# S5 parameters kept on chip, raw gates in DRAM, and another preparation of y in a two-layer trunk on one Trainium2 core

## The chip, the core and the metric

The kernel runs on one core of one Trainium2 chip. The metric is the time of one execution on the device, in microseconds (us). TensorE (PE) does the matmuls, VectorE (DVE), ScalarE (ACT) and GpSimd (POOL) the element-wise work, and SyncE (SP) issues most of the DMAs; ScalarE issues a few. Each engine runs its own instructions in the order in which they stand in its program, and waits at one until the semaphores it needs are there; so does SP with its DMAs.

## What is computed

Two layers over x of 1024 frames by 1024 channels, all fp32. Layer 0 is an S5 state-space mixer with a GLU behind it, layer 1 a spatial gating unit.

```python
for i in range(DEPTH):                      # DEPTH = 2
    h = rmsnorm(x, norm_g[i])
    if i % 2 == 0:
        branch, gate = jnp.split(h @ s5_w_in[j], 2, axis=-1)
        y = jax.nn.gelu(s5_mixer(branch, A_re, A_im, log_dt, B_re, B_im, C_re, C_im, D))
        y = y * jax.nn.sigmoid(y @ s5_w_glu[j] + s5_b_glu[j])
        out = (y * jax.nn.silu(gate)) @ s5_w_out[j]
    else:
        u, v, gate = jnp.split(h @ sgu_w_in[j], 3, axis=-1)
        y = sgu_mixer(jax.nn.gelu(u), jax.nn.gelu(v), ln_g, ln_b, w_s, b_s)
        out = (y * jax.nn.silu(gate)) @ sgu_w_out[j]
    x = x + out
return rmsnorm(x, final_g)
```

`s5_mixer` runs 64 groups of 16 channels; each drives 64 complex diagonal states (`lam_bar = exp(lam * dt)`) over the frames and gives `Re(C h) + D u`.

## The kernel before

Every large product is done in three matmuls per pair of 128-row operands, because each fp32 operand is split in a high and a low part (L104 to L106: high by high, low by high, high by low). The unit of work is a *half*: one tile of 128 output channels for 512 of the 1024 frames, 8 x 3 = 24 matmuls into one PSUM bank. A weight tile is loaded by SP into `raw` (L135), its high part is made by ScalarE (`w_hi`, L138) and its low part by VectorE or GpSimd (`w_lo`, L109).

*Stage 1* is the S5 input projection: 16 tiles of two halves. Tiles 0 to 7 are the branch, 8 to 15 the gate. `in_out` (L470) empties a bank: VectorE multiplies by the row norm `rb`; a branch half goes to `stage` and from there to DRAM (`u_d`), a gate half also goes through ScalarE's Silu (L479) and to `sg_d`. Two banks, `mm`, take turns for these halves.

The *head* of stage 1 (about the first 90 us) also loads and transposes x (`x_tiles`, `x_norm`) and makes the parameters of the state space on VectorE and GpSimd (`s5_params`): powers of `lam_bar` (`lp`), of the input weights (`mu`), phase tables (`eb`, `ea16`) and scaled B and C. They are written to DRAM (`g_d`, eight DMAs; `b_d`).

Beside the halves run 16 *units* of four groups each. `gen` makes two tables on VectorE (`wn`, `xn`) from a piece of `g_d` loaded back as `gp`, of which ScalarE copies a part to a PSUM bank (`gq`, L544). `gen_pe` transposes `wn` on PE (`wt`) and makes a strip of Toeplitz taps, `kpad`; a DMA writes it skewed to DRAM (`t_d`), another reads it back (`traw`), and ScalarE copies it in another order of columns (`toep`, L601). `ssm_in` loads `us`, multiplies on PE into a bank `rot`, rotates and scans on VectorE, GpSimd and ScalarE (`gg`, `hh`), with a second bank of `rot` for the swapped state. `ssm_out` multiplies `toep` and `xn` with `us` and `hh`; ScalarE copies the result (`ysb`) and issues its store to `y_d`.

The list `todo` sets in which order these pieces and the halves are written; a scheduler then orders each engine's instructions within the limits of the dependences, so the programs' rows shown below, not the list alone, tell what stands behind what.

*Preparation of y.* `prep(k)` loads tile k of `y_d` in one DMA (L715), applies the gelu on ScalarE in two halves (L721), and splits it into `hi` and `lo` on VectorE (L723, `sub_hi`); it also loads `sg_d[k]`, multiplies it with the gelu and writes `p_d[k]`. Tiles 0 to 2 are prepared from `todo`, in the pool `B0`; tiles 3 to 7 after the list, in `B1`, which takes the place of the units' memory.

*GLU.* For each of eight tiles: a weight tile, two halves from all eight `hi`/`lo` pairs in four `mm` banks, a sigmoid on ScalarE, a product with `p_d[i]` loaded back, and the split into `ahi`, `alo` for the output projection. Behind it come the second layer's stages.

The lines on which the order around the change rests (`EARLY` is 3, `KT` 8):

```python
    for k in range(EARLY):
        todo.append((max([t_gen] + [e[0] for e in todo if e[2:] == ("out", 2 * k + 1)]) + PREP, 9, "prep", k))
...
    for e in todo:
        run[e[2]](e[3])
    wk_cm.__exit__(None, None, None)
    held_cm.__exit__(None, None, None)
...
    w_next = in_w[16]
    for k in range(EARLY, KT):
        prep(k)
```

Of the kernel before, what the change touches and what calls it, by code (L numbers as in the profile page):

```python
# [63 lines left out]
def trunk(ctx, tc, x, norm_g, final_g, s5_w_in, A_re, A_im, log_dt, B_re, B_im, C_re, C_im,  # L64
# [209 lines left out]
    def s5_params():  # L274
# [102 lines left out]
        eb = per.tile([P, 2, 32, 17], F32, name="eb")  # L377
        ea16 = per.tile([P, 2, 32, 8], F32, name="ea16")
        te = xp.tile([P, 32, 8], F32, name="te")
        for e, size, lo in ((eb, 17, G), (ea16, 8, G + 32)):  # L380
            GP.memset(e[:, 0, :, 0:1], 1.0)
            GP.memset(e[:, 1, :, 0:1], 0.0)
            for i, a in ((0, cth), (1, sth)):
                GP.tensor_copy(e[:, i, :, 1:2], a[:, lo:lo + 32].unsqueeze(2))
            k = 1
            while k < size - 1:
                w = min(k, size - 1 - k)
                cmul(GP, e[:, 0, :, k + 1:k + 1 + w], e[:, 1, :, k + 1:k + 1 + w],
                     e[:, 0, :, 1:1 + w], e[:, 1, :, 1:1 + w],
                     e[:, 0, :, k:k + 1].broadcast_to([P, 32, w]), e[:, 1, :, k:k + 1].broadcast_to([P, 32, w]),  # L390
                     te[:, :, 0:w])
                k += w
# [579 lines left out]
```

## Time and profile before

| | us |
|---|---|
| median of 3 runs (902.65 to 907.44) | 904.67 |
| profiled execution, its own time | 903.87 |
| its span in the trace | 902.2 |
| PE busy in the span | 831.6 (92%) |
| VectorE, ScalarE, GpSimd busy | 494.1, 306.5, 233.0 |
| granted clock of PE, mean | 0.976 of full |

The time lies 1.67 us around the span. A busy share is an average over stages with different limits, so it is read stage by stage: the windows show where PE is full and where it stands. For each stretch in which it stands, the waits tell which instruction of which engine came last, and the timeline of that engine (or of SP's queue) tells what that instruction stood behind. Matmuls are pipelined: one is recorded with about 0.39 us, but the next starts 0.23 us after it at full clock.

### The profile page before, as it was taken

Reading aid. Unit: us, or ns where it says so; the run is one execution under the profiler, and the core shown is the slowest. Engines: PE = TensorE matmul, PEld = TensorE weight load, DVE = VectorE, ACT = ScalarE, POOL = GpSimd, SP = SyncE. Lnnn points to the kernel's source line nnn. Section 1 sums busy time; section 2 is a strip of 40 time slices with the busy share of each in tenths; the row PEclk is TensorE's granted clock in tenths of the full one; section 3 lists DMA queues with packets and bytes.
Section 4 is the critical chain, followed back from the end, with each engine's and each line's share of the span. In section 5 each row is a group of like instructions: output and inputs, shape, how many; then the busy total and the mean of one; then the engine's idle time right before and its main releaser. Section 6 shows DMA issues by size and latency. Waiting matters only on the chain.

```text
span 902.2 us, 10797 instructions
## 1 busy us (share of the span) xinstructions
PE 831.6 (92%) x3946; PEld 673.1 (75%) x3946; DVE 494.1 (55%) x1097; ACT 306.5 (34%) x523; POOL 233.0 (26%) x262
## 2 busy tenths in 40 slices
PE   6978988999898758999999999999999899999996
PEld 5756867777777546888888888888888688888884
DVE  3896597786575556334417721121279964552155
ACT  5511244545555545334312232221221122242122
POOL 1085875656532100000000000000016731212221
PEclk9989999999999988999999999999999999999999
DMA  9827678898776698335402231230130011352022
GB/s 247 166 94 205 193 203 240 238 237 225 224 208 199 217 379 294 111 128 186 153 14 80 94 117 47 70 94 1 37 103 1 1 47 47 139 165 69 1 94 93
DMA packets 135621, 123.24 MB, mean 137 GB/s; under 512 B 23696, under 2 KB 112784, under 8 KB 135568
## 3 DMA queue, kind: packets, MB, share of 16 engines
q1 hardware_dynamic: 123664, 107.87, 40.5%
q10 hardware_dynamic: 11904, 14.68, 4.7%
q8 instruction: 31, 0.51, 0.2%
q14 instruction: 22, 0.18, 0.1%
HBM read 75.87 MB, written 37.75 MB: 126 GB/s over the span
## 4 chain that ended last, share of the span: by engine, by line
PE 58%; DVE 15%; DMA 15%; ACT 4%; POOL 4%; SPq 3%; issue 2%; ACTq 0%; DVEq 0%; POOLq 0%
PE mm L104 18%; PE mm L106 18%; PE mm L105 18%; DMA gp<-g_d 3%; DMA c<-y_d 3%; DMA t_d<-kpad 2%; DVE lo L886 2%; PE aux L910 1%; DMA traw<-t_d 1%; DVE lo L887 1%; DMA xh<-in_x 1%; POOL w_lo L109 1%; DMA raw<-in_sgu_w_in 1%; DVE tv L560 1%; ACT c L721 1%
## 5 line engine op out<-in xcount | busy, mean ns | idle before, releaser
L104 PE MATMUL mm<-ahi,w_hi 128*128 128x512 f32 x512 | 207.9, 407 | 14.0 <-DVE stage L475 8.6
L106 PE MATMUL mm<-ahi,w_lo 128*128 128x512 f32 x512 | 205.5, 402 | 0.0
L105 PE MATMUL mm<-alo,w_hi 128*128 128x512 f32 x512 | 204.7, 400 | 0.0
L104 PEld LDWEIGHTS mm<-ahi,w_hi 128*128 128x128 f32 x512 | 98.3, 192 | 35.0 <-issue 9.2
L105 PEld LDWEIGHTS mm<-alo,w_hi 128*128 128x128 f32 x512 | 98.5, 192 | 21.1 <-issue 0.8
L106 PEld LDWEIGHTS mm<-ahi,w_lo 128*128 128x128 f32 x512 | 98.2, 192 | 21.4 <-DVE w_lo L109 0.5
L138 ACT ACTIVATE w_hi<-raw 128x1024 fp32r<-128x1024 f32 x39 | 41.2, 1057 | 113.0 <-PE mm L105 73.1
L888 POOL TENSOR_TENSOR lo<-lo,lnb 128x128 f32<-128x128 f32 x64 | 34.3, 566 | 162.6 <-DVE lo L887 162.6
L109 DVE TENSOR_TENSOR w_lo<-raw,w_hi 128x1024 fp32r<-128x1024 f32 x25 | 36.6, 1464 | 63.7 <-ACT w_hi L138 63.7
L104 PE MATMUL mm<-hi,w_hi 128*128 128x512 f32 x128 | 51.9, 416 | 15.1 <-DVE hi L723 13.3
L847 POOL TENSOR_SCALAR_AFFINE_SELECT wsn<-wsn 128x1024 f32<-128x1024 f32 x1 | 1.1, 1093 | 223.3 <-DMA wsn<-in_sgu_w_s 223.3
L105 PE MATMUL mm<-lo,w_hi 128*128 128x512 f32 x128 | 52.2, 407 | 0.0
L106 PE MATMUL mm<-hi,w_lo 128*128 128x512 f32 x128 | 51.8, 407 | 0.0
L106 PE MATMUL mm<-hi,alo 128*128 128x512 f32 x128 | 51.0, 399 | 0.0
L104 PE MATMUL mm<-hi,ahi 128*128 128x512 f32 x128 | 50.7, 396 | 0.0
L104 PE MATMUL mm<-ahi,hi 128*128 128x512 f32 x128 | 50.6, 396 | 0.0
L105 PE MATMUL mm<-lo,ahi 128*128 128x512 f32 x128 | 50.6, 395 | 0.0
L105 PE MATMUL mm<-alo,hi 128*128 128x512 f32 x128 | 50.6, 395 | 0.0
L105 PE MATMUL mm<-c,ahi 128*128 128x512 f32 x128 | 50.5, 395 | 0.0
L106 PE MATMUL mm<-c,alo 128*128 128x512 f32 x128 | 50.5, 395 | 0.0
L106 PE MATMUL mm<-ahi,lo 128*128 128x512 f32 x128 | 50.4, 395 | 0.0
L104 PE MATMUL mm<-c,ahi 128*128 128x512 f32 x128 | 50.1, 396 | 0.0
(255 smaller groups left out, 1509.8 us busy)
## 6 DMA issues: line engine op xcount, KB each, us to landing
raw<-in_sgu_w_in SPq DMA_DIRECT2D x24, 512.0 KB, 3.7
cs<-e SPq DMA_DIRECT2D x32, 256.0 KB, 4.5
t_d<-kpad SPq DMA_DIRECT2D x16, 512.0 KB, 4.6
raw<-in_s_w_in SPq DMA_DIRECT2D x15, 512.0 KB, 5.8
u_d<-stage ACTq DMA_DIRECT2D x8, 512.0 KB, 3.8
us<-u_d SPq DMA_DIRECT2D x16, 256.0 KB, 5.4
traw<-t_d SPq DMA_DIRECT2D x16, 256.0 KB, 3.0
y_d<-ysb ACTq DMA_DIRECT2D x16, 256.0 KB, 4.2
```

Source lines behind the costliest of these rows:

```text
L104: T.matmul(ps, lhsT=ah, rhs=bh, start=first, stop=False)
L105: T.matmul(ps, lhsT=ah, rhs=bl, start=False, stop=False)
L106: T.matmul(ps, lhsT=al, rhs=bh, start=False, stop=last)
L109: eng.tensor_tensor(lo, src, hi.bitcast(F32), ALU.subtract)
L138: S.activation(hi, raw, AF.Copy)
L560: V.tensor_tensor(tv, pw[1].unsqueeze(2).broadcast_to(sh), second.unsqueeze(3).broadcast_to(sh), ALU.mult)
L721: S.activation(gy.rearrange("p (c l) -> p c l", l=L), yt.rearrange("p (l c) -> p c l", l=L)[:, half * 64:(half + 1) * 64], AF.Gelu_apprx_tanh)
L847: GP.affine_select(wsn, wsn, pattern=[[0, 8], [-1, P]], compare_op=ALU.is_ge, fill=0.0, base=0, channel_multiplier=1)
L886: V.tensor_scalar(vs[h][:, n], vs[h][:, n], mv[:, 0:1], r[:, 0:1], ALU.subtract, ALU.mult)
L887: V.tensor_tensor(vs[h][:, n], vs[h][:, n], lng[:, h * P:(h + 1) * P], ALU.mult)
L888: GP.tensor_tensor(vs[h][:, n], vs[h][:, n], lnb[:, h * P:(h + 1) * P], ALU.add)
L910: T.matmul(ps[:, i * P:(i + 1) * P], lhsT=vs[h][:, half * 4 + i], rhs=wtm[:, h], start=True, stop=True)
```

## The change

It has seven parts.

- The loads of A and of `log_dt` go first, on ScalarE's queue (`load_a`); the rest of the parameters is loaded by SP (`load_bc`). One `x_norm` does both halves of the frames. The first four halves run in four banks before the first is emptied.
- `bn`, `bs`, `ca`, `cb`, `lp` and `mu` stay in SBUF (pool `per`); `g_d` and `gp` are gone. `gq` is copied from `lp` and `mu` by two ScalarE copies. `mu` is one complex product of 128x512; the phase tables are one table, `ph`. The sign of `bs` is applied by ScalarE.
- The swapped state is written into the bank that `ssm_in` already has (`gw = pv`).
- `t_d` is written by four DMAs of 16 rows per unit, in a layout in which `traw` is used as it is loaded; the `toep` copy is gone.
- A gate half is stored raw (`z_d`); Silu, as z times sigmoid(z), is done in the GLU. `sg_d` and `p_d` are gone. `hi + lo` is used for y there.
- `y_d` has another layout, and `prep` loads a tile with eight DMAs of 16 rows.
- `todo` now has a "shut2" that closes the units' pools and opens `B1`, and "prep" entries for k = 3 to 7 behind it. The loop over k = 3 to 7 after the list is as it was.

Two loads of the second layer (`bsb`, `gb2`) share a buffer with `gb`.

```diff
-    banks, bank_n = {"mm": [0, 1], "aux": [2, 3, 4, 5, 6, 7]}, {}
+    banks, bank_n = {"mm": [0, 1, 2, 3], "aux": [4, 5, 6, 7]}, {}
...
-            V.tensor_scalar(dr, ident, r[:, b:b + 1], None, ALU.mult)
...
+                S.activation(dr, ident, AF.Copy, scale=r[:, half * 4 + b:half * 4 + b + 1])
...
-        V.tensor_scalar(bs, bs, sgn[:, 0:1], None, ALU.mult)
+        S.activation(bs, bs, AF.Copy, scale=sgn[:, 0:1])
...
-        for i, src in ((0, ca), (1, cb), (2, bn), (3, bs)):
-            Q.dma_start(g_d[:, :, i * P:(i + 1) * P].rearrange("b p x -> p b x"),
-                        src.rearrange("p (b g) h -> p b (g h)", g=8))
...
+        sh = [P, G, L]
+        cmul(V, mu[:, 0], mu[:, 1], lp[:, 0, :, 1:], lp[:, 1, :, 1:], br.unsqueeze(2).broadcast_to(sh),
+             bi.unsqueeze(2).broadcast_to(sh), tb)
...
-            V.tensor_tensor(ps, ps, rb[:, hs], ALU.mult)
-            S.activation(st[:, hs], ps, AF.Silu)
+            V.tensor_tensor(st[:, hs], ps, rb[:, hs], ALU.mult)
...
     p00 = in_mm(0, 0)
+    p10 = in_mm(1, 0)
+    x_tiles(1, range(KT))
     a_params()
-    x_norm(0)
+    x_norm()
+    p01 = in_mm(0, 1)
     in_out(0, 0, p00)
...
-        gps[b] = wg.tile([P, 6 * P], F32, name="gp", bufs=nb["gp"])
-        Q.dma_start(gps[b], g_d[b])
-        gqs[b] = bank("gq")
-        S.activation(gqs[b][:, 0:2 * P], gps[b][:, 4 * P:6 * P], AF.Copy)
+        gqs[b] = bank("gq")[:, 0:4 * 64].rearrange("p (i r g l) -> p i r g l", i=2, r=2, g=8)
+        S.activation(gqs[b][:, 0], lp[:, :, gs, 0:L], AF.Copy)
+        S.activation(gqs[b][:, 1], mu[:, :, gs], AF.Copy)
...
-        Q.dma_start(t_d[u].rearrange("g j m x -> (g j) m x"),
-                    bass.AP(kp.tensor, kp.offset, [kp.ap[0], (HG, L), (1, P)]))
+        for i in range(UG):
+            k_ = kp[i * JR:i * JR + HG]
+            Q.dma_start(t_d[u][i], bass.AP(k_.tensor, k_.offset, [k_.ap[0], (HG, L), (1, P)]))
...
-        tts[u] = wk.tile([P, UG, HG, L], F32, name="toep", bufs=nb["toep"])
-        S.activation(tts[u], traw.rearrange("p g (l h) -> p g h l", h=HG), AF.Copy)
+        tts[u] = traw
...
-        gw = bank("rot").rearrange("p (g c) -> p g c", g=UG)
+        gw = pv
...
+    t_y = max(e[0] for e in todo if e[2] == "out")
+    todo.append((t_y, 10, "shut2", None))
+    for k in range(EARLY, KT):
+        todo.append((t_y, 10 + k, "prep", k))
...
-        Q.dma_start(yt, y_d[k].rearrange("g h l c -> (g h) (l c)"))
+        for g in range(8):
+            Q.dma_start(yt[g * HG:(g + 1) * HG].rearrange("p (l c) -> p l c", l=L), y_d[k][g].rearrange("l h c -> h l c"))
...
-        sgt = ctile()
-        Q.dma_start(sgt, sg_d[k])
-        V.tensor_tensor(sgt, gt, sgt, ALU.mult)
-        Q.dma_start(p_d[k], sgt)
...
-        sig, yv = ctile(), ctile()
-        Q.dma_start(yv, p_d[i])
+        sig, zt, yv = ctile(), ctile(), ctile()
+        Q.dma_start(zt, z_d[i])
         for half in range(2):
             hs = slice(half * HALF, (half + 1) * HALF)
+
+            V.tensor_tensor(yv[:, hs], bh[i][:, hs].bitcast(F32), bl[i][:, hs].bitcast(F32), ALU.add)
+            S.activation(sig[:, hs], zt[:, hs], AF.Sigmoid)
+            V.tensor_tensor(yv[:, hs], yv[:, hs], zt[:, hs], ALU.mult)
+            V.tensor_tensor(yv[:, hs], yv[:, hs], sig[:, hs], ALU.mult)
```

SP's queue around the loads of the last unit, before: `t_d15`, `us` and `traw` are unit 15's, `raw` is the weight of GLU tile 0, `c<-y_d0` the first load of a preparation. The numbers behind names tell buffers and DRAM tiles apart.

```order
L594 DMA cs_2516<-e_2261 64x1024
L586 DMA t_d15_162<-kpad1_111 1024x1x128
L607 DMA us_2644<-u_d7_138 128x4x128
L135 DMA raw_2857<-in_s5_w_glu 128x8x128
L599 DMA traw_2600<-t_d15_162 128x4x128
L715 DMA c_2524<-y_d0_139 128x1024
L726 DMA c_2535<-sg_d0_115 128x1024
L728 DMA p_d0_163<-c_2535 128x1024
```

And after, the same place (`us_2563` and `traw_2522` are unit 15's):

```order
L703 DMA c_2438<-y_d0_143 16x8x128 x8
L572 DMA t_d14_165<-kpad0_114 128x1x128 x4
L584 DMA traw_2383<-t_d14_165 128x4x128
L703 DMA c_2456<-y_d1_144 16x8x128 x7
L572 DMA t_d15_166<-kpad1_115 128x1x128 x4
L703 DMA c_2456<-y_d1_144 16x8x128
L591 DMA us_2563<-u_d7_142 128x4x128
L135 DMA raw_2865<-in_s5_w_glu 128x8x128
L584 DMA traw_2522<-t_d15_166 128x4x128
L703 DMA c_2474<-y_d2_145 16x8x128 x8
L703 DMA c_2733<-y_d4_147 16x8x128 x8
L135 DMA raw_3097<-in_s5_w_glu 128x8x128
```

The loads of y tiles 0 and 1 moved ahead of unit 15's loads, and each tile is eight DMAs instead of one. What follows on SP after that, up to the weight of GLU tile 1 (`raw_3021`; `raw_3097` is that of tile 2):

```order
L703 DMA c_2715<-y_d3_146 16x8x128 x8
L703 DMA c_2751<-y_d5_148 16x8x128 x8
L703 DMA c_2769<-y_d6_149 16x8x128 x8
L703 DMA c_2787<-y_d7_150 16x8x128 x8
L703 DMA c_2931<-y_d3_146 16x8x128 x8
L703 DMA c_2949<-y_d4_147 16x8x128 x8
L703 DMA c_2967<-y_d5_148 16x8x128 x8
L703 DMA c_2985<-y_d6_149 16x8x128 x8
L703 DMA c_3003<-y_d7_150 16x8x128 x8
L135 DMA raw_3021<-in_s5_w_glu 128x8x128
L737 DMA c_3028<-z_d0_119 128x1024
```

Tiles 3 to 7 of y stand there a second time, into other buffers, and the weight of GLU tile 1 moved behind all of them.

PE at the start of the GLU, with the last y tile (k = 7), before: `mm_3014` and `mm_3043` are the two halves of GLU tile 0, `mm_3081` and `mm_3110` those of tile 1.

```order
L104 MATMUL mm_3014<-hi7_2993,w_hi_2859 128x512
L104 MATMUL mm_3081<-hi7_2993,w_hi_3007 128x512
L105 MATMUL mm_3014<-lo7_2994,w_hi_2859 128x512
L106 MATMUL mm_3014<-hi7_2993,w_lo_2860 128x512
L105 MATMUL mm_3081<-lo7_2994,w_hi_3007 128x512
L106 MATMUL mm_3081<-hi7_2993,w_lo_3008 128x512
L104 MATMUL mm_3043<-hi7_2993,w_hi_2859 128x512
L104 MATMUL mm_3110<-hi7_2993,w_hi_3007 128x512
```

After, the same place: `mm_3035` and `mm_3068` are tile 0, `mm_3111` and `mm_3144` tile 1, and `hi7_3013` is the second set's.

```order
L104 MATMUL mm_3035<-hi7_3013,w_hi_2867 128x512
L105 MATMUL mm_3035<-lo7_3014,w_hi_2867 128x512
L106 MATMUL mm_3035<-hi7_3013,w_lo_2868 128x512
L104 MATMUL mm_3068<-hi7_3013,w_hi_2867 128x512
L104 MATMUL mm_3111<-hi0_2448,w_hi_3023 128x512
L105 MATMUL mm_3111<-lo0_2449,w_hi_3023 128x512
L104 MATMUL mm_3144<-hi0_2448,w_hi_3023 128x512
L105 MATMUL mm_3144<-lo0_2449,w_hi_3023 128x512
L105 MATMUL mm_3068<-lo7_3014,w_hi_2867 128x512
L106 MATMUL mm_3068<-hi7_3013,w_lo_2868 128x512
L106 MATMUL mm_3111<-hi0_2448,w_lo_3024 128x512
```

Before, the matmuls of the two tiles alternate for each y tile; now tile 1 begins, with y tile 0, where tile 0 is all but done.

## Rows read from the trace of the kernel before

**Rows 1.** Windows: from:to and length in us, busy us (instructions) by engine, PEclk, DMA, GB/s.
```profile
0.00:90.00 90.00, 70.67 (x312) 56.05 (x313) 66.19 (x194) 30.60 (x47) 33.81 (x67) 0.94 0.70 178
...
112.50:292.00 179.50, 160.14 (x955) 130.11 (x954) 129.06 (x234) 92.63 (x147) 99.70 (x76) 0.98 0.80 224
292.00:360.00 68.00, 48.52 (x185) 36.94 (x184) 42.02 (x63) 35.81 (x42) 2.56 (x2) 0.85 0.84 290
360.00:700.00 340.00, 340.00 (x1505) 276.07 (x1504) 138.09 (x365) 92.17 (x194) 19.52 (x36) 1.00 0.26 83
```

**Rows 2.** Timeline of PE, head: start, us, operation, count [idle before and what ended it].
```profile
55.21 0.76 PE L104 MATMUL mm<-ahi,w_hi 128*128 128x512 f32 x1 [4.27 <-DVE stage L475]
...
72.38 0.47 PE L104 MATMUL mm<-ahi,w_hi 128*128 128x512 f32 x1 [3.96 <-DVE stage L475]
```

**Rows 3.** Timeline of DVE in the head.
```profile
60.32 4.46 DVE L168 TENSOR_TENSOR t<-t,t 128x128 f32<-128x128 f32 x2
...
74.01 0.29 DVE L168 TENSOR_TENSOR t<-t,t 128x128 f32<-128x128 f32 x1
...
87.53 0.69 DVE L559 TENSOR_TENSOR wn<-gq,gp 128x512 f32<-128x512 f32 x1 [1.09 <-ACT gq L544]
```

**Rows 4.** Waits of PE, 112.5 to 302 us: total, times, longest.
```profile
PE mm L104 <- ACT stage L479: 5.4, 2, 4.3
PE rot L612 <- DMA us<-u_d: 2.6, 1, 2.6
...
PE rot L612 <- DVE gg L623: 1.7, 3, 1.0
...
PE aux L580 <- ACT kpad L584: 1.1, 1, 1.1
```

**Rows 5.** Groups of ACT, 112.5 to 345: busy, mean ns | idle before, releaser.
```profile
L601 ACT ACTIVATE toep<-traw 128x512 f32<-128x512 f32 x16 | 17.6, 1100 | 37.0 <-DMA traw<-t_d 37.0
```

**Rows 6.** The page, part 5: the two halves of a weight tile.
```profile
L138 ACT ACTIVATE w_hi<-raw 128x1024 fp32r<-128x1024 f32 x39 | 41.2, 1057 | 113.0 <-PE mm L105 73.1
...
L109 DVE TENSOR_TENSOR w_lo<-raw,w_hi 128x1024 fp32r<-128x1024 f32 x25 | 36.6, 1464 | 63.7 <-ACT w_hi L138 63.7
```

**Rows 7.** Chain of waits, 296 to 346 us: start, us, what.
```profile
319.88 5.66 DMA c<-y_d
...
328.09 10.07 DMA c<-y_d
...
341.09 0.43 PE mm L105
...
343.07 0.23 PE mm L105
```

**Rows 8.** Timeline of PE, from the last gates into the GLU.
```profile
301.43 0.51 PE L104 MATMUL mm<-ahi,w_hi 128*128 128x512 f32 x1 [4.34 <-ACT stage L479]
...
308.04 0.48 PE L104 MATMUL mm<-ahi,w_hi 128*128 128x512 f32 x1
...
339.87 1.22 PE L104 MATMUL mm<-hi,w_hi 128*128 128x512 f32 x2 [7.76 <-DVE hi L723]
...
351.60 0.50 PE L104 MATMUL mm<-hi,w_hi 128*128 128x512 f32 x1 [1.76 <-ACT w_hi L138]
```

**Rows 9.** Timeline of SP's queue (SPq): start, us of issue, DMA, count.
```profile
0.81 1.81 SPq L204 DMA_DIRECT2D xh<-in_x  x4
...
278.33 1.13 SPq L607 DMA_DIRECT2D us<-u_d  x1
...
331.78 0.32 SPq L715 DMA_DIRECT2D c<-y_d  x1
```

**Rows 10.** DMA issues, 112 to 292 us: count, KB each, median us to landing.
```profile
sg_d<-stage ACTq DMA_DIRECT2D x6, 512.0 KB, 3.8
...
b<-b_d SPq DMA_DIRECT2D x6, 128.0 KB, 2.7
```

**Rows 11.** DMA issues, 292 to 345 us.
```profile
c<-y_d SPq DMA_DIRECT2D x7, 512.0 KB, 7.9
raw<-in_s_w_glu SPq DMA_DIRECT2D x3, 512.0 KB, 7.4
```

More of the change, by code (lines that the diff above doesn't have):

```diff
@@ L241, in trunk @@
     ldt = tmp()
-    bn = tmp((P, G, HG))
-    bs = tmp((P, G, HG))
+    bn, bs, ca, cb = (per.tile([P, G, HG], F32, name=c) for c in ("bn", "bs", "ca", "cb"))
+    lp = per.tile([P, 2, G, L + 1], F32, name="lp")
+    mu = per.tile([P, 2, G, L], F32, name="mu")
     cnat = xp.tile([P, KT, 3, NS], F32, name="cnat")
@@ L374, in s5_params @@
         tt(sth, sth, t2, ALU.add)
[L377 to L392, printed above, removed]
+        ph = per.tile([P, 2, 64, 17], F32, name="ph")
+        te = xp.tile([P, 64, 8], F32, name="te")
+        GP.memset(ph[:, 0, :, 0:1], 1.0)
+        GP.memset(ph[:, 1, :, 0:1], 0.0)
+        for i, a in ((0, cth), (1, sth)):
+            GP.tensor_copy(ph[:, i, :, 1:2], a[:, G:2 * G].unsqueeze(2))
+        for k, n in ((1, 64), (2, 64), (4, 64), (8, 32)):
+            cmul(GP, ph[:, 0, 0:n, k + 1:2 * k + 1], ph[:, 1, 0:n, k + 1:2 * k + 1],
+                 ph[:, 0, 0:n, 1:k + 1], ph[:, 1, 0:n, 1:k + 1],
+                 ph[:, 0, 0:n, k:k + 1].broadcast_to([P, n, k]), ph[:, 1, 0:n, k:k + 1].broadcast_to([P, n, k]),
+                 te[:, 0:n, 0:k])
         for kp in kpad:
@@ L451, in s5_params @@
         Q.dma_start(b_d.rearrange("b p x -> p b x"), b0.rearrange("p (b g) h -> p b (g h)", g=8))
-        return dict(dt=dskip, ea=ea, eb=eb, ea16=ea16)
-    sg_d = [drp.tile([P, D], F32, name=f"sg_d{i}") for i in range(8)]
+        return dict(dt=dskip, ea=ea, eb=ph[:, :, 0:32], ea16=ph[:, :, 32:64, 0:8])
+    z_d = [drp.tile([P, D], F32, name=f"z_d{i}") for i in range(8)]
     x1_d = [drp.tile([P, D], F32, name=f"x1_d{i}") for i in range(8)]
     u_d = [drp.tile([8, HG, L, NC], F32, name=f"u_d{i}") for i in range(8)]
-    y_d = [drp.tile([8, HG, L, NC], F32, name=f"y_d{i}") for i in range(8)]
-    t_d = [drp.tile([4, JR, L, P], F32, name=f"t_d{i}") for i in range(16)]
-    p_d = [drp.tile([P, D], F32, name=f"p_d{i}") for i in range(8)]
-    g_d = drp.tile([KT, P, 6 * P], F32, name="g_d")
+    y_d = [drp.tile([8, L, HG, NC], F32, name=f"y_d{i}") for i in range(8)]
+    t_d = [drp.tile([4, HG, L, P], F32, name=f"t_d{i}") for i in range(16)]
     b_d = drp.tile([KT, P, 8 * JR], F32, name="b_d")
@@ L483, in in_out @@
             else:
-                S.dma_start(sg_d[i - 8], st)
+                S.dma_start(z_d[i - 8], st)
     def in_half(i, half):
@@ L526, in trunk @@
     U4 = [P, UG, NC]
-    tabs, wns, wts, xns, b0s, css, tts, us, hhs, gps, gqs = ({} for _ in range(11))
-    banks.update(aux=[2, 3], rot=[4, 5], gq=[6], tv=[7])
+    tabs, wns, wts, xns, b0s, css, tts, us, hhs, gqs = ({} for _ in range(10))
+    banks.update(mm=[0, 1], aux=[2, 3], rot=[4, 5], gq=[6], tv=[7])
     def gen_tab(b):
@@ L596, in gen_toep @@
     def gen_toep(u):
[L598 to L601 removed]
+        traw = wk.tile([P, UG, P], F32, name="traw", bufs=nb["toep"])
+        Q.dma_start(traw, t_d[u].rearrange("g j m x -> (j m) g x"))
+        tts[u] = traw
     def ssm_in(u):
@@ L930, in trunk @@
         load_panel(sgu_w_out[0], half * HALF, a_hi, a_lo, half * HALF)
+        if half == 0:
+            gb2 = late.tile([P, D], F32, name="gb2", tag="gb")
+            Q.dma_start(gb2, final_g.partition_broadcast(P))
         for n in range(KT):
```

124 lines of the change are left out of this document (53 added, 71 removed).

## The prediction

> **What bounds the kernel now.** I read the stages first. PE is full from 360 to 700 us and works 70.67 of the first 90 us, 160.14 of the 179.5 us up to 292, and 48.52 of the 68 us up to 360 [rows 1]; its granted clock in that last stretch is 0.85. After 700 the change moves only two small loads, which have slack. So whatever the change is worth comes out of 19.3 idle us in the head (0 to 90), 19.4 in the middle and 19.5 at the start of the GLU, and out of the clock lost beside them. The second view is what PE waited for in each stretch. In the head two waits of 4.27 and 3.96 us end with VectorE's copy of a finished half out of its bank (L475) [rows 2]: VectorE is then inside the parameter arithmetic, with two 128x128 operations in 4.46 us where the same line later takes 0.29, and the first unit's `wn` is made only at 87.53 [rows 3]. In the middle there are many short waits, and most of them end on ScalarE or on what stands behind it: 5.4 us for L479 (the Silu that empties a bank) is the first line, 1.1 for `kpad` the last; VectorE's `gg` has 1.7 and one load of `us` 2.6 [rows 4]. ScalarE itself did 17.6 us of `toep` copies and stood 37.0 us in front of them until `traw` landed, with all that is queued behind [rows 5]. In the GLU's start the chain of waits names one thing, the loads `c<-y_d`: 5.66 and 10.07 us in a row, and PE starts again at 339.87 [rows 7, 8].
>
> Three instants are used below. In the program's order, unit 15's last output matmul ends at T0 = 308.04, with ten matmuls of the last gate half behind it. PE finishes GLU tiles 0 and 1 and begins tile 2 at 351.60, which is T0 + 43.6 [rows 8]. From there PE is full in both kernels if the GLU keeps its pace.
>
> **Head: -4.5 us.** The change takes the parameters' loads first, keeps them on chip, drops the eight `g_d` writes and the `gp` loads, makes `mu` in six operations instead of 24, and gives the first halves four banks. With four banks halves (0,0), (1,0), (0,1), (1,1) run without an evacuation, so the first wait (4.27, and its clock loss) goes. The clock loss I price from the chain: between 339.87 and 343.07 a matmul took 0.43 us instead of 0.23 [rows 7, 8], so 3.2 x (1 - 0.23/0.43) = 1.5 us per long wait. The same VectorE chain still has to run before `mu`, and the scaling of `bs` moves to ScalarE, where the last copies of x queue behind its load. So I keep the second wait: 4.27 + 1.5 = 5.8 at most for one wait, 11.2 for both, less a bit for ScalarE's new queue: -4.5, bounds -1 and -9.
>
> **Middle: -5.5, and -5.8 for one wait at 301 us.** The `toep` copies go (17.6 us of ScalarE), the `gq` copies stop waiting for a load, Silu leaves stage 1, and the rotation uses one bank less per unit. Waits of PE that end on ScalarE come to 17.2 us in this stretch (eight of twelve lines [rows 4]). The largest, 4.34 us for the Silu at 301.43 [rows 8], goes whole, with its clock: -5.8. Of the other 12.9 I take less than half, because a short wait removed often only shows the next link (load of `us`, `gg`, then `hh`): -5.5, bounds 0 and -12. New on this path are four `t_d` issues per unit instead of one. At a pitch of 0.46 us (four x loads in 1.81 [rows 9]) that is 1.4 us more on SP per unit, against half the bytes and the copy of 1.1 us that no longer follows: nothing.
>
> **Unit 15: +2.** In the program's order the loads of `y_d0` and `y_d1` now stand ahead of `t_d15`, of unit 15's `us` and of its `traw`: 16 issues, 7.4 us, and the second group waits for a gelu. Before, `us` went out at 278.33 [rows 9] and unit 15's output ended 30 us later, so most of this is slack: 0 to +8, I take +2.
>
> So T0' = 308.0 - 4.5 - 5.5 - 5.8 + 2.0 = 294.2; and because 21 matmuls of the last half now follow unit 15's output instead of ten, 11 x 0.23 = 2.5 earlier again: T0' = 291.7.
>
> **Start of the GLU: the preparation of y happens twice.** The new list entries prepare tiles 3 to 7 after `shut2`, but the old loop `for k in range(EARLY, KT): prep(k)` is still there and prepares the same five again, into other buffers, and it is these that the GLU's matmuls read. Each preparation also issues eight loads of 64 KB instead of one of 512 KB. So of what is "beside the last gates" nothing is used, and SP has 104 y loads to issue where it had eight. Along SP from T0': the seventh load of `y_d5` waits on a semaphore that the store of `z_d7` last used. That store needs the last half (T0' + 4.8), VectorE's evacuation (0.7 [rows 3]) and its landing (3.8, as `sg_d` had [rows 10]) with 0.3 of issue: T0' + 9.6. Behind it stand 58 y loads: 58 x 0.46 = 26.7, T0' + 36.3. Only then comes the weight of GLU tile 1: issue 0.5, landing 5.0 (before: 7.4 beside full DMA engines [rows 11]; less with small loads), its high part 1.1 and its low part 1.5 [rows 6]: T0' + 44.4. The last y tile lands and is split before that. PE's order puts all of tile 0 ahead of tile 1 and no longer mixes them, so about 46 matmuls are left: 10.6 + 1.5 for the clock. Tile 2 begins at T0' + 56.5 = 348.2, and its weight was loaded early. Against 351.60 that is -3.4.
>
> **The gates** cost an addition and two products of VectorE per half in the GLU (0.69 each [rows 3]) and one more sigmoid, in a stretch where VectorE works 138 of 340 us [rows 1]; `sg_d` and `p_d`, 16 MB written and read, become `z_d` with 8. Nothing, while PE's 11 us per tile cover it; were that cover gone, 2 x 3 x 0.69 = 4.1 us a tile.
>
> **Sum**, against the profiled execution's 903.87 us (902.2 of span and 1.67 around it; the median of the runs is 0.8 higher): 903.87 - 3.4 = **900.5 us**.
>
> One rule of the Trainium skill speaks against this edit: "DMA: Bandwidth & Descriptors", Rules for kernel authors, wants many small transfers coalesced into one and calls those under 64 KB mostly overhead. Its fit in Anatomy of one DMA gives about 2.1 us for 64 KB, an estimate; no row here shows such a load, the nearest (128 KB, 2.7 us) agrees. By that figure eight semaphores would allow a load each 0.27 us, so SP's issue would stay the limit and the first rival below would fall.
>
> **Rivals.**
> (a) *Slower: landing, not issue, paces the y loads.* SP's DMAs use eight semaphores in turn, so a load can't be issued before the one eight earlier has landed. From a landing of 8 x 0.46 = 3.7 us on, that sets the pace. For it: `c<-y_d` had 7.9 us at 512 KB [rows 11]; against it: `b`, 128 KB, has 2.7 [rows 10]. At 5.4 us the pitch is 0.68, 58 x 0.22 = 12.5 more: 913. Chance 0.18.
> (b) *Slower: unit 15 starves* behind the y loads: the whole 8 us instead of 2, and its gelu holds up `rot<-gg` on ScalarE: 906.5 to 909. Chance 0.12.
> (c) *Faster: the middle's waits go almost whole.* Without the 37 us in front of `toep` ScalarE runs ahead of PE; only the waits for `us` and `gg` stay. Then -12 instead of -5.5, and -9 in the head: 889.5. Chance 0.20.
> (d) *Faster: the y loads go out at 0.32 us*, as one of them did [rows 9]: 58 x 0.14 = 8.1 less, 892.5. Chance 0.08.
> That the change doesn't do what it says is part of the forecast: without the second preparation 40 issues would fall away, 18.4 us, and the time would be near 882.
>
> **Chances and range.** The forecast has 0.42, and its own range is 896 to 905. About 0.5% (4.5 us) is what a measurement of this kernel can tell from no change. Faster by more: (c), (d) and not quite half of the forecast, 0.44; within: the rest of it and half of (b), 0.30; slower: (a), the rest of (b) and some unknown, 0.26. Eight in ten: from beyond (c), 886, to past (a), 917.
>
> **What would show it.** Right: PE has no wait on a bank's evacuation before 60 us and none near 300 on ScalarE; SP issues `c<-y_d` 104 times, for some 27 us without another kind of load after unit 15; PE idles about 15 us after `mm<-hi2` and then does six matmuls per y tile; tile 1's first matmul waits for `w_hi`. Wrong: if that weight lands before the last y load, if y loads land in over 4 us, if the head's two waits stand as they were, or if PE waits over 3 us for unit 15's `us` or `traw`.

## The result, and the profile of the changed kernel

The changed kernel takes **915.52 us** (median of four runs, 914.27 to 916.85), the kernel before 905.45 in the runs beside it: ratio 1.0114, 95% interval 1.0081 to 1.0146. The forecast was 900.5 and faster; the range holds the time, the sign is wrong. The profiled execution is the 914.27 one, span 912.3, so 10.4 us over the 903.87 from which the sum was made.

The windows of the changed kernel, cut as in [rows 1] (from:to and length, busy us of PE, PEld, DVE, ACT, POOL with their instructions, PEclk, DMA share, GB/s):

```profile
0.00:90.00 90.00, 69.38 (x310) 55.79 (x311) 64.62 (x157) 33.48 (x57) 32.98 (x48) 0.92 0.53 140
112.50:292.00 179.50, 156.42 (x930) 128.26 (x929) 121.55 (x235) 71.33 (x126) 99.91 (x76) 0.94 0.75 192
292.00:360.00 68.00, 45.69 (x165) 32.57 (x164) 42.78 (x74) 35.46 (x42) 2.60 (x2) 0.75 0.60 167
360.00:700.00 340.00, 340.00 (x1504) 276.02 (x1503) 154.32 (x365) 98.79 (x201) 13.01 (x25) 1.00 0.27 88
```

ScalarE has 21.3 us less to do in the middle and the DMA engines have less to move, as the change says; and yet PE works less there (156.42 against 160.14 us), less in the head and less at the GLU's start, and its mean granted clock is lower each time (0.92, 0.94 and 0.75 against 0.94, 0.98 and 0.85). After 360 us it is full again. What PE waited for, from 112 to 302 us and then from 302 to 362 us (engine, line, what it waited for: total, times, longest):

```profile
PE rot L596 <- DMA us<-u_d: 20.9, 7, 8.9
PE aux L564 <- DVE kpad L569: 1.0, 2, 0.8
...
PE rot L596 <- ACT rot L610: 0.3, 1, 0.3
```

```profile
PE mm L104 <- DVE hi L711: 20.4, 4, 17.7
PE mm L105 <- DVE lo L109: 0.8, 1, 0.8
PE mm L104 <- DVE stage L460: 0.4, 1, 0.4
```

Beside [rows 4] this is a swap of names: the waits that ended on ScalarE have gone, down to 0.3 us, and the load of `us`, which had 2.6 us in one wait, has 20.9 us in seven. The totals of the two lists hardly differ (23.2 us before, 23.6 after). Lines of PE's timeline place the rest (start, us, operation, count, [idle before and what ended it]); the last is the first matmul of the projection behind the GLU:

```profile
251.82 2.08 PE L596 MATMUL rot<-us,wt 128*128 128x128 f32 x8 [8.91 <-DMA us<-u_d]
...
306.09 0.48 PE L104 MATMUL mm<-ahi,w_hi 128*128 128x512 f32 x1
...
333.02 0.79 PE L104 MATMUL mm<-hi,w_hi 128*128 128x512 f32 x1 [17.66 <-DVE hi L711]
...
349.44 0.80 PE L104 MATMUL mm<-hi,w_hi 128*128 128x512 f32 x1 [1.53 <-DVE hi L711]
...
431.16 0.39 PE L104 MATMUL mm<-hi,ahi 128*128 128x512 f32 x1
```

and the same first matmul in the kernel before:

```profile
420.77 0.39 PE L104 MATMUL mm<-hi,ahi 128*128 128x512 f32 x1
```

In the prediction's terms T0' is 306.09, where it had 291.7 (before: 308.04 [rows 8]). GLU tile 2 begins at 363.96: the 288 matmuls of tiles 2 to 7, at the 0.2333 us from one to the next that PE shows there, end at 431.16. That is T0' + 57.9, where the prediction had 56.5. Nearly the whole miss, 14.4 us, lies ahead of T0', in head and middle.

### The profile page after: what moved, and what is told of

Its sections match the earlier page's. It is cut to its first block, busy times and chain, and to the rows that moved or that the text cites. A ratio compares the mean times of both kernels' runs of the same rounds, so it can differ in the third digit from the quotient of the medians.

```text
span 912.3 us, 11000 instructions
## 1 busy us (share of the span) xinstructions
PE 834.2 (91%) x3946; PEld 674.9 (74%) x3946; DVE 515.7 (57%) x1120; ACT 297.4 (33%) x529; POOL 232.1 (25%) x240
## 4 chain that ended last, share of the span: by engine, by line
PE 58%; DVE 15%; DMA 12%; SPq 5%; POOL 5%; ACT 2%; issue 2%; ACTq 0%; DVEq 0%; POOLq 0%
PE mm L104 18%; PE mm L106 18%; PE mm L105 18%; DMA cs<-e 4%; SPq L703 2%; DVE lo L877 2%; DMA c<-y_d 2%; DMA us<-u_d 2%; PE aux L901 1%; DVE lo L878 1%; SPq L572 1%; DMA xh<-in_x 1%; DMA t_d<-kpad 1%; DVE stage L457 1%; DMA raw<-in_sgu_w_in 1%
## 5 line engine op out<-in xcount | busy, mean ns | idle before, releaser
L104 PE MATMUL mm<-hi,w_hi 128*128 128x512 f32 x128 | 53.8, 422 | 20.4 <-DVE hi L711 20.4
L138 ACT ACTIVATE w_hi<-raw 128x1024 fp32r<-128x1024 f32 x39 | 41.2, 1056 | 92.9 <-PE mm L105 71.3
L109 POOL TENSOR_TENSOR w_lo<-raw,w_hi 128x1024 fp32r<-128x1024 f32 x14 | 33.7, 2404 | 67.1 <-DVE stage L457 44.8
L105 PE MATMUL mm<-c,ahi 128*128 128x512 f32 x128 | 50.5, 395 | 0.0
```

The costliest lines, as they stand in the source:

```text
L104: T.matmul(ps, lhsT=ah, rhs=bh, start=first, stop=False)
L105: T.matmul(ps, lhsT=ah, rhs=bl, start=False, stop=False)
L109: eng.tensor_tensor(lo, src, hi.bitcast(F32), ALU.subtract)
L138: S.activation(hi, raw, AF.Copy)
```

## Experiments

Twelve more kernels ran. The table reads each profiled execution at two instants: the start of unit 15's last output product, and PE's first product of the GLU, which comes when the gate matmuls left behind unit 15 are done. What follows, up to the span's end, is the GLU and the later stages; the later stages, from the first matmul of the projection behind the GLU, take 479.1 to 483.3 us in all fourteen. Gains and losses below are differences of the ratios, since each kernel ran beside its own runs of the kernel before (medians 903.69 to 905.45). The profiled execution of and_bs_pool is the slowest of its four, 868.63 us.

| kernel | median us | ratio to before, 95% | unit 15's last output product | first GLU product | from there to the end |
|---|---|---|---|---|---|
| before | 905.45 | 1 | 307.9 | 310.2 | 592.0 |
| after | 915.52 | 1.0114 [1.0081, 1.0146] | 306.0 | 311.0 | 601.3 |
| one_prep | 895.69 | 0.992 [0.989, 0.9949] | 301.7 | 306.8 | 587.0 |
| one_t_store | 899.66 | 0.9955 [0.9934, 0.9976] | 293.4 | 300.2 | 597.2 |
| us_on_act | 905.07 | 1.0028 [1.0005, 1.0051] | 293.4 | 301.3 | 601.7 |
| bs_dve | 911.60 | 1.0094 [1.0062, 1.0126] | 306.4 | 311.4 | 600.6 |
| b_dve | 896.82 | 0.9923 [0.9897, 0.995] | 287.4 | 304.0 | 590.5 |
| y_two_queues | 924.01 | 1.0208 [1.0167, 1.0248] | 310.6 | 314.3 | 608.7 |
| three_undone | 867.18 | 0.9597 [0.9557, 0.9636] | 276.8 | 286.6 | 577.7 |
| and_bs_pool | 862.47 | 0.9555 [0.9516, 0.9595] | 279.9 | 289.5 | 577.2 |
| all_and_b_dve | 866.40 | 0.957 [0.954, 0.9599] | 272.9 | 292.8 | 571.9 |
| before_four_t_stores | 910.47 | 1.0077 [1.005, 1.0104] | 316.5 | 319.1 | 589.4 |
| before_eight_y_loads | 925.30 | 1.0221 [1.0184, 1.0258] | 308.5 | 310.5 | 612.8 |
| before_b_dve | 907.71 | 1.003 [1.0009, 1.0051] | 311.0 | 314.0 | 593.9 |

**The second preparation of y**, taken out of the changed kernel:

```diff
-    for k in range(EARLY, KT):
-        prep(k)
```

> The changed kernel without the loop that prepares y tiles 3 to 7 a second time; the GLU reads the first set. Theory A (SP's issue of y loads sets the GLU's start): 40 of the 72 loads in a row that took 39.59 us in the changed kernel fall away, 40 x 0.55 = 22 us of SP; what is left behind the store of z_d7 is 18 loads, about 10 us, then the weight of tile 1, its split and some 46 matmuls. GLU tile 2 begins 16 to 20 us earlier: 896 to 900 us. Rival B (ScalarE's gelu and the store of the last unit's y set the start, the second set is hidden in them): under 6 us less, 910 or more. Rival C (the weight of tile 1 is late for another reason): 904 to 909.

895.69 us: 0.992/1.0114 is 1.9% under the changed kernel, 17.5 us, where the prediction's aside had 18.4. SP's queue in the changed kernel, from the last gates on (start, us for the group, DMA, count):

```profile
290.49 13.12 SPq L703 DMA_DIRECT2D c<-y_d  x16
305.53 0.39 SPq L135 DMA_DIRECT2D raw<-in_s_w_glu  x1
306.03 39.59 SPq L703 DMA_DIRECT2D c<-y_d  x72
345.67 0.43 SPq L135 DMA_DIRECT2D raw<-in_s_w_glu  x1
346.21 0.99 SPq L737 DMA_DIRECT2D c<-z_d  x2
```

and without the second preparation:

```profile
301.29 0.39 SPq L135 DMA_DIRECT2D raw<-in_s_w_glu  x1
301.80 19.98 SPq L703 DMA_DIRECT2D c<-y_d  x32
321.83 0.43 SPq L135 DMA_DIRECT2D raw<-in_s_w_glu  x1
```

72 loads in a row become 32, and PE's 17.66 us in front of y3, the first tile that is prepared twice, are gone (its longest wait for `hi` is 1.3 us). By the table 14.3 us of the span's 18.5 fall after the first GLU product. The other 4.2 fall before unit 15's output, where the program's order is the same in both; its waits for `us` came to 16.2 instead of 20.9 us. Why, this run doesn't tell.

**Four stores of the Toeplitz blocks, or one.** The changed kernel with a store of the whole `kpad` per unit, and `traw` reading its first half of rows:

```diff
-    t_d = [drp.tile([4, HG, L, P], F32, name=f"t_d{i}") for i in range(16)]
+    t_d = [drp.tile([4, JR, L, P], F32, name=f"t_d{i}") for i in range(16)]
...
-        for i in range(UG):
-            k_ = kp[i * JR:i * JR + HG]
-            Q.dma_start(t_d[u][i], bass.AP(k_.tensor, k_.offset, [k_.ap[0], (HG, L), (1, P)]))
+        Q.dma_start(t_d[u].rearrange("g j m x -> (g j) m x"),
+                    bass.AP(kp.tensor, kp.offset, [kp.ap[0], (HG, L), (1, P)]))
...
-        Q.dma_start(traw, t_d[u].rearrange("g j m x -> (j m) g x"))
+        Q.dma_start(traw, t_d[u][:, 0:HG].rearrange("g j m x -> (j m) g x"))
```

> The changed kernel with one store of t_d per unit over all 128 rows, as before, instead of four of 16 rows; the Toeplitz blocks are still used as loaded. Theory A (48 more issues on SP delay the loads of us behind them): PE's 20.9 us of waits for us between 112 and 302 us fall below 12, and the time by 6 to 10: 906 to 910. Rival B (us stands in SP's order behind a t_d that waits for kpad and a traw that waits for t_d, however many DMAs these are): waits for us stay over 17, time within 3 of 915.5.

899.66 us, 14 under the changed kernel, though it stores twice the bytes. PE's waits for `us` fall from 20.9 to 11.8 us. Unit 15's output comes 12.6 us earlier, and the first GLU product 10.8; the rest of the 12.6 is gates that now stand behind unit 15. The chain of waits of the changed kernel ahead of its 8.91 us shows how a store can delay a load that has nothing to do with it (start, us, what):

```profile
232.50 0.88 SPq L572
...
233.42 1.34 SPq L572
...
234.82 0.59 SPq L572
...
235.45 5.42 DMA t_d<-kpad
...
241.04 0.37 SPq L584
...
241.85 0.37 SPq L135
...
242.33 0.60 SPq L579
...
242.97 0.61 SPq L579
...
243.62 8.15 DMA us<-u_d
...
251.82 2.08 PE rot L596 x8
```

L572 is the stores, four in 4.79 us; L584 is `traw`, which waits on SP until the last of them has landed; behind it stand a weight, two `cs` loads, and only then `us` (L591), which goes out at once when its turn comes. In the kernel before, the store of a unit is one issue of 0.56 us.

Three things bound what this shows. Of the 8.91 us the load's own time from issue to landing is 8.15, where the median of the loads of `us` in this stretch is 5.6 us. SP's standing for `t_d` to land did not grow: from 112 to 302 us it comes to 17.9 us, and to 41.2 in the kernel before; what grew is the issuing, four times 0.60 us (median) instead of 0.56. And the edit moves other issues too: two loads of `us` stand directly behind each other on SP three times in this stretch of the changed kernel, twice with one store, never in the kernel before. How much of the 14 us is the stores and how much is that order, this run doesn't part.

**`us` moved out of that queue** to ScalarE's:

```diff
-        Q.dma_start(us[u], u_d[b][o:o + UG].rearrange("g j m c -> (j m) g c"))
+        S.dma_start(us[u], u_d[b][o:o + UG].rearrange("g j m c -> (j m) g c"))
```

> The changed kernel with the loads of us issued by ScalarE instead of SP. Rival B of the run before (us is late because of what stands ahead of it in SP's order): PE's waits for us fall from 20.9 to under 8 us and the time by 8 to 14, 902 to 908, unless ScalarE now stands in front of the load. Theory C (the units' pace is set elsewhere, by GpSimd and the loads of cs, and PE's wait only changes its name): the sum of PE's waits in the middle stays between 18 and 26 us, time 912 to 918.

905.07 us, 8 under the changed kernel. The waits for `us` fall to 6.8 us with a longest of 3.2. Unit 15's output is again 12.6 us earlier, the first GLU product 9.7; other short waits appear (3.1 for `ysb`, 5.7 for `kpad` in three lines). At the GLU's start it gives nothing: the wait for `hi` is 18.1 us, since the y loads are still 104.

**The same two costs put into the kernel before**, one at a time. Four stores, of half the rows each (the block that `traw` reads stays the same):

```diff
-        Q.dma_start(t_d[u].rearrange("g j m x -> (g j) m x"),
-                    bass.AP(kp.tensor, kp.offset, [kp.ap[0], (HG, L), (1, P)]))
+        for i in range(UG):
+            k_ = kp[i * JR:i * JR + HG]
+            Q.dma_start(t_d[u][i, 0:HG], bass.AP(k_.tensor, k_.offset, [k_.ap[0], (HG, L), (1, P)]))
```

> The kernel before with one part of the change alone: t_d stored by four DMAs of 16 rows per unit instead of one over 128 rows. Theory A (48 more issues on SP delay what stands behind them there): PE waits for us 8 to 15 us more in the middle, 911 to 918. Rival (SP stood 41 us for t_d to land anyway and the smaller stores land earlier, so it is even): 901 to 907, waits of PE as before.

910.47 us: ratio 1.0077, 7 us slower, all of it ahead of unit 15's output (8.6 us later). Neither theory holds: the price is smaller than in the changed kernel, and it doesn't show at `us` (0.7 us in all) but at `gg` and `toep` (5.9 and 2.8 us, where they had 1.7 and 1.1). Why `us` has slack there no run tells: in the kernel before too it often stands directly behind a `traw` on SP, at 250.79 us for one. Eight y loads per tile, in the layout that the kernel before has:

```diff
-        Q.dma_start(yt, y_d[k].rearrange("g h l c -> (g h) (l c)"))
+        for g in range(8):
+            Q.dma_start(yt[g * HG:(g + 1) * HG], y_d[k][g].rearrange("h l c -> h (l c)"))
```

> The kernel before with one part of the change alone: eight y loads per tile instead of one, still one preparation. Theory A (SP's issue is the pace at the start of the GLU): 56 loads more x 0.5 us = 28 us, of which the waits for c<-y_d in the chain (10.07 and 5.66 us) hide a part; 912 to 922. Rival (the DMA engines, full at 373 GB/s there, are the pace in that kernel): 902 to 908.

925.30 us, 20 slower than before, 2.2%, and more than expected. All of it lies behind the first GLU product (612.8 against 592.0 us). So even one preparation costs that much when each load is split in eight; here they stand among the loads and stores of `sg_d` and `p_d`, and SP also waits between them for the products that it stores.

**The head.** The sign of `bs`, made by VectorE instead of ScalarE:

```diff
-        S.activation(bs, bs, AF.Copy, scale=sgn[:, 0:1])
+        V.tensor_scalar(bs, bs, sgn[:, 0:1], None, ALU.mult)
```

> The changed kernel with the sign of bs applied by VectorE again, as before. Theory A (in the head ScalarE stands 7.11 us at that scaling until bs has landed, and with it the last copies of x, of the norm and so VectorE): VectorE's idle of 7.92 us near 32 to 40 us falls to under 3, PE's wait of 8.68 us at 76.8 to under 4, and the first unit's tables come 5 us earlier; if the units keep that, 909 to 911. Rival B (VectorE's parameter chain is as late anyway, since it runs beside GpSimd's long operations): the wait at 76.8 stays over 7, 914 to 917.

911.60 us, 0.2% under the changed kernel, with intervals that overlap. PE's longest wait in the head is 7.36 us, at 77.46: not under 4, as theory A had it. The trace says why it is so little. First the two groups of the changed kernel, ACT and DVE (busy, mean ns | idle before and what ended it; the line L215 is that of DVE's timeline), then DVE's group with the edit:

```profile
L303 ACT ACTIVATE bs<-bs,t 128x1024 f32<-128x1024 f32 x1 | 1.1, 1147 | 7.1 <-DMA bs<-bn 7.1
```

```profile
39.73 0.75 DVE L215 SCALAR_TENSOR_TENSOR alo<-aux,g,ahi 128x512 fp32r<-128x512 f32 x1 [7.92 <-ACT ahi L214]
```

```profile
L303 DVE TENSOR_SCALAR bs<-bs,t 128x1024 f32<-128x1024 f32 x1 | 0.8, 752 | 7.3 <-DMA bs<-bn 7.3
```

ScalarE stood 7.1 us for the load of `bs`, with a copy of x behind it, and VectorE stood 7.92 us for that copy. With the edit VectorE stands 7.3 us for the load itself. The wait moved with the instruction. In the fastest version it is on GpSimd (below): there `mu` is done at 81.9 us instead of 84.3, and PE's longest head wait is 5.92 instead of 8.68 us.

Three products of B moved from GpSimd to VectorE, because VectorE's 128x128 steps beside them are slow (the last section):

```diff
-        GP.tensor_tensor(bv, br.unsqueeze(2).broadcast_to(shb), bn, ALU.mult)
-        GP.tensor_tensor(b1, bi.unsqueeze(2).broadcast_to(shb), bs, ALU.mult)
-        GP.tensor_tensor(bv, bv, b1, ALU.add)
+        V.tensor_tensor(bv, br.unsqueeze(2).broadcast_to(shb), bn, ALU.mult)
+        V.tensor_tensor(b1, bi.unsqueeze(2).broadcast_to(shb), bs, ALU.mult)
+        V.tensor_tensor(bv, bv, b1, ALU.add)
```

> The changed kernel with the three 128x1024 operations that make the scaled B (L432 to L434) on VectorE instead of GpSimd. Theory H (an operation of VectorE that meets a 128x1024 operation of GpSimd in the head ends only with it: six between 49 and 75 us took 1.7 to 2.5 us instead of 0.3 to 0.6): three of the six go back to under 0.7 us, the three added ones cost 1.2 each, PE's wait of 8.68 us at 76.8 falls to about 6, the time is 911 to 915. Rival (these six are long by themselves): they stay, the added work comes on top, the wait grows to 11 to 12, 916 to 920.

896.82 us, 17 under the changed kernel, and not for the reason tried: `mu` is done later (88.1 against 84.3 us), and the head's longest wait is 7.6 us. What moved is the program's order, which follows times that the kernel works out for its engines when it is built: the units stand earlier among the gates. Unit 0 enters at 97.4 instead of 105.8 us, one and a half halves, and unit 15's last output product comes at 287.4, with 16.6 us of gates behind it instead of 5.0, two halves more. Under these the y tiles are loaded: PE's long wait is 7.49 us instead of 17.66. That is 10.2 of the 10.8 us gained behind the first GLU product. Another 7.0 us come ahead of it, of which 3.9 are shorter waits in the middle; the rest isn't accounted for. The same edit in the kernel before, where the end of that order, ten matmuls behind unit 15, doesn't change:

> The kernel before with the edit of e5 (the three operations that make the scaled B on VectorE). Its program has unit 15's output ten matmuls before the end of stage 1, as without the edit, while in e5 the edit moved it from 21 to 70. Theory O (e5 gained by that order: the units run 1.5 halves earlier beside the gates): here nothing to gain, 901 to 908. Theory H (GpSimd's long operations hold VectorE in the head): VectorE's two operations of 2.2 us become short and the head ends earlier, 893 to 899.

907.71 us, no gain. Unit 0 enters earlier there too (97.3 instead of 102.9 us), and PE then waits longer for `kpad` and `gg` (7.2 and 6.1 us from 112 to 302 us, where it had 2.3 and 1.7). So the products by themselves don't gain. That the order behind unit 15 does, because it hides a long queue of y loads, fits the rows of both kernels; no run moved the order alone.

**All three undone at once**: one preparation, one store, `us` on ScalarE's queue (the three diffs above).

> The changed kernel with one preparation of y, one store of t_d per unit, and us issued by ScalarE, that is e1, e3 and e4 together. If the three add (they are 1.9, 1.6 and 0.9% of the kernel before): 0.967 of it, 875 us. If e3 and e4 free the same waits for us and only the larger counts: 0.976, 882 us. If the GLU's start falls back on the next limit (the gelu, the last store of y): 885 to 890.

867.18 us: ratio 0.9597, better than the 0.967 that the three alone make as a product. Up to the first GLU product the three alone add up (4.2 + 10.8 + 9.7 = 24.7 us, measured 24.4). The surplus is behind it: 9.8 us of gates now stand behind unit 15, and the few y loads fit under them. The waits of PE from 112 to 302 us:

```profile
PE mm L104 <- DVE hi L710: 3.0, 2, 2.1
PE aux L623 <- DMA traw<-t_d: 2.9, 1, 2.9
PE rot L595 <- DMA us<-u_d: 2.5, 1, 2.5
```

The first line belongs to the GLU, which begins at 286.6 here; the middle and the last gates together now wait some 7.5 us, where the kernel before had, by the prediction's sum, 17.2 us on ScalarE alone [rows 4, 8]. Then the sign of `bs` on GpSimd too:

```diff
-        S.activation(bs, bs, AF.Copy, scale=sgn[:, 0:1])
+        GP.tensor_scalar(bs, bs, sgn[:, 0:1], None, ALU.mult)
```

> As e7, and the sign of bs applied by GpSimd, which is idle until 48 us, so that neither ScalarE nor VectorE stands at its load. If the head's stand of ScalarE costs the time that e2 showed (0.2%): 1 to 3 us under e7. If now the head is on the path of a middle that no longer waits for us: 3 to 6 us under e7. If neither: the same as e7.

**862.47 us**, ratio 0.9555 [0.9516, 0.9595]: the fastest version, 4.5% under the kernel before, though not separable from the one ahead of it. And the products of B on VectorE on top of that:

> e8 with the edit of e5. In its program unit 15's output stands 83 matmuls before the end of stage 1 instead of 41. Theory O: y is prepared beside these, 42 x 0.23 = 9.7 us at most, of which e8 still had 3 to 6 us of PE's waits at the end of the gates: 855 to 860. Rival (e8's rest of idle time is in the head, which the edit lengthens for VectorE): 861 to 866.

866.40 us, no further gain, as the rival had it, 0.4 us past its range. Unit 15's output is 3.9 us earlier than with three edits undone and 19.9 us of gates stand behind it, but the first GLU product comes 6.3 us later and what follows is only 5.8 us shorter. With the units earlier PE waits for `kpad` (5.6 us in one wait), as in the kernel before with the same edit, and of the y loads little was left to hide.

**Two issuers for the y loads**, the second preparation kept:

```diff
-            Q.dma_start(yt[g * HG:(g + 1) * HG].rearrange("p (l c) -> p l c", l=L), y_d[k][g].rearrange("l h c -> h l c"))
+            (Q if g % 2 else GP).dma_start(yt[g * HG:(g + 1) * HG].rearrange("p (l c) -> p l c", l=L), y_d[k][g].rearrange("l h c -> h l c"))
```

> The changed kernel, second preparation included, with every other y load issued by GpSimd instead of SP. Theory A (SP's 0.55 us per issue is the pace of the 72 loads in a row): SP has 36 of them, about 20 us instead of 39.6, and GLU tile 2 starts 12 to 18 us earlier, 898 to 904. Rival D (the pace is the landing of the loads, 2.7 us with eight in flight, or the DMA engines): the 72 loads still take over 33 us, 910 to 916. Rival E (GpSimd's issue is slower than SP's): its 36 loads take over 36 us, 910 or more.

924.01 us, 0.9% over the changed kernel. Theory A fell, and of rival D only the sign came: the last 72 loads still took some 48 us. Rival E's figures came, GpSimd's 36 loads from 303.67 to 350.71 us, but its reason only in part: an issue takes GpSimd 0.53 us, 19 us for 36, and in the rest it stood. The DMA issues from 292 us on (count, KB each, median us to landing), first of the changed kernel, then with two issuers, then that kernel's window and PE's waits:

```profile
c<-y_d SPq DMA_DIRECT2D x85, 64.0 KB, 2.7
```

```profile
c<-y_d POOLq DMA_DIRECT2D x41, 64.0 KB, 7.6
c<-y_d SPq DMA_DIRECT2D x40, 64.0 KB, 7.7
```

```profile
292.00:360.00 68.00, 43.95 (x191) 35.59 (x189) 31.58 (x57) 27.59 (x31) 24.12 (x43) 0.78 0.92 157
```

```profile
PE mm L104 <- ACT w_hi L138: 20.0, 2, 18.7
PE mm L104 <- DVE hi L711: 10.5, 2, 5.8
```

The landing time nearly triples, the DMA engines are busy 0.92 of the stretch instead of 0.60 and move no more (157 against 167 GB/s), and PE's longest wait is now for the weight of a GLU tile, issued among the y loads at 326.71 and landed 9.5 us later. The Trainium skill, "DMA: Bandwidth & Descriptors", section Issuing engines are not separate DMA queues, says that issuing from several engines saves only the sequencer's issue time; this run agrees that it brought no bandwidth. Whatever issue time it saved was lost: partly to landing, partly to GpSimd's own order, for GpSimd stood 10.9 us for a gelu and 8.3 us for a store of y among its loads. The run doesn't part the two.

## Why the prediction was wrong, step by step

- **Start of the GLU: right in its course, with errors that partly cancel.** 56.5 us forecast, 57.9 measured. The second preparation, SP's issue as its limit, tile 1's weight behind the last y loads, and PE's long wait behind `mm<-hi2` are all there. Part by part, the store of `z_d7` landed where the forecast had it: issued at 312.27, landed 3.9 us later, and the next y load went out at 316.20, T0' + 10.1 (forecast 9.6). The 58 loads from there on took 29.4 us, not 26.7: mostly 0.43 us of issue, one beginning 0.47 us after the other, with a few longer. The weight took 6.6 us from its issue to its low part, not 8.1, and was split at 352.31, T0' + 46.2, where the sum had 44.4. One sign failed: PE does not wait for that weight. Its last wait is 1.53 us for the last y tile, at 349.44, and the weight was ready just behind it, so the sum's last step named the wrong one of two things that came within 3 us of each other. Rival (a) fell: a y load landed in 2.7 us (median), under the 3.7 from which it decides. So did rival (d), with 0.47 and not 0.32 us a load. The rule that the prediction set against the edit, from the Trainium skill's "DMA: Bandwidth & Descriptors", Rules for kernel authors, agrees with what the undone splits and the added ones measured: 14 us for one store instead of four, 20 for eight y loads instead of one. The fit that it took from Anatomy of one DMA on the same page of the Trainium skill, 2.1 us for 64 KB, is stated there for DMAs that GpSimd issues; these loads were SP's and landed in 2.7.
- **Middle: the step that failed.** It had two terms, -5.5 and -5.8 for the wait at 301 us, and both mechanisms came: no wait of PE on ScalarE is over 0.3 us from 112 to 302 us, and at 303.82 PE waits 0.43 us where it had 4.34 [rows 8]. But the sentence that priced the four `t_d` issues per unit at "nothing" was wrong. It counted 1.4 us on SP's queue (four issues of 0.60 instead of one of 0.56 make 1.8) and set them against a saved copy on ScalarE, a different engine; it didn't say what is queued on SP behind these issues and behind the wait of `traw` for the last store. That was `us`, and PE waited 20.9 us for it. Undone, this one edit gives back 14 us, and moving `us` alone to another queue 8; put into the kernel before, it costs 7. So the term measures 7 to 14 us where the sum had nothing; the part of it that is the changed order of SP's queue stays open.
- **Head: -4.5 became about +1.** PE works 69.38 us of the first 90 where it worked 70.67 [rows 1]. The first wait went as said: up to 60 us PE waits for no bank to be emptied. The second was to stay at 3.96 us and grew to 8.68, and one of 2.70 for x's copy behind the sign of `bs` came, which the prediction mentions ("the last copies of x queue behind its load") and prices at "a bit". `mu` in six operations was done at 84.3 us, where VectorE's parameter chain had ended at 78.3; the first unit's `wn` still began a little earlier, at 86.24 instead of 87.53 us [rows 3]. Two experiments on this gave 0.2% and 0.4%, both within their intervals; that VectorE waits for `bs` and is slow beside GpSimd is read from rows, what else holds `mu` is open.
- **Unit 15: about right.** Its waits for `us` and `traw` were 1.60 and 0.7 us, +2 forecast. Rival (b) fell.
- **Sum.** Head, middle and unit 15 together were -13.8 in the forecast. In the trace T0' - T0 is -1.95, of which -2.5 is the order of the last gates, so they gave +0.6. That difference of 14.4 us is the miss. The GLU's start adds 1.4. Against it stand 2.0 us that the forecast left out: it took PE as full from 351.60 on, but in the kernel before the 288 matmuls from there to 420.77 took 69.17 us, 2.0 more than at full clock, behind a wait that the changed kernel doesn't have there. 900.5 + 14.4 + 1.4 - 2.0 is 914.3, beside the 914.27 of the profiled execution.
- **Rival (c)** had the middle's waits go almost whole and 889.5. It named `us` as a wait that stays, and not as one that grows. With the queue mended and one preparation its mechanism does come, at 867.
- The aside that the time would be near 882 without the second preparation came out at 895.69: 13 too low, the same 14 us from the middle.

## What to carry to other kernels

A DMA that is split into several is paid for not by the engine whose work it saves but by whatever stands in the same queue behind its issues and behind the next instruction that waits for the last piece: write down that queue in order, to the first load that a full engine needs, before calling the extra issues free. When an expected gain is missing, compare the waits by name: here those removed and those that came were nearly equal, 23.2 and 23.6 us in the middle, so that only the names told them apart. And an edit that gains for another reason than its own (the products of B) should be tried where that reason is absent.

## What the runs showed of the hardware that was not expected

Loads of 64 KB issued by SP alone landed in 2.7 us (median), and in 7.6 and 7.7 us when GpSimd issued every other one, with the DMA engines' share up from 0.60 to 0.92 at fewer GB/s (157 against 167).

VectorE's small steps take several times as long beside a large operation of GpSimd. From the two engines' timelines in the changed kernel (first VectorE, then GpSimd):

```profile
64.45 2.06 DVE L167 TENSOR_TENSOR t<-lp 128x128 f32<-128x128 f32 x1
...
72.17 2.45 DVE L167 TENSOR_TENSOR t<-lp 128x256 f32<-128x256 f32 x1
74.55 0.62 DVE L169 TENSOR_TENSOR lp<-lp 128x256 f32<-128x256 f32 x1
```

```profile
63.60 2.76 POOL L432 TENSOR_TENSOR t<-t,bn 128x1024 f32<-128x1024 f32 x1 [2.09 <-DVE t L414]
...
71.94 2.40 POOL L434 TENSOR_TENSOR t<-t,t 128x1024 f32<-128x1024 f32 x1
```

Each long step of VectorE ends with the operation of GpSimd beside it, and the next one of the same size takes 0.62 us. This is the pattern of [rows 3] too, where two such steps took 4.46 us beside two operations of GpSimd that began at 60.22 and 62.65 us. The run with the products of B on VectorE bears it out, though its gain went elsewhere: the two steps shown above, with no large operation of GpSimd beside them, took 0.84 and 0.83 us, and a smaller one that met GpSimd's split of a weight took 2.52 (VectorE, then GpSimd):

```profile
66.89 2.52 DVE L170 TENSOR_TENSOR t<-lp 128x64 f32<-128x64 f32 x1
...
72.69 0.84 DVE L167 TENSOR_TENSOR t<-lp 128x128 f32<-128x128 f32 x1
...
80.68 0.83 DVE L167 TENSOR_TENSOR t<-lp 128x256 f32<-128x256 f32 x1
```

```profile
66.85 2.40 POOL L109 TENSOR_TENSOR w_lo<-raw,w_hi 128x1024 fp32r<-128x1024 f32 x1
```
